# Thirteen pairs per feed-forward network as seven block products, with parts of 7, 8 and 7 pairs

## The chip, the cores and the metric

The kernel runs on one core of one Trainium2 chip. The metric is the time of one execution on the device in microseconds (us), as the median of several runs; smaller is better. The engines are TensorE (PE in the profile; its weight loads are PEld), VectorE (DVE), ScalarE (ACT), GpSimd (POOL) and SyncE (SP), which only issues transfers here. POOL issues transfers too.

## The reference

Two layers of a decoder trunk work on 16 meta tokens and 512 tokens, 528 rows of 1024 numbers, in float32. Each layer has a mixer (attention, a long and a short convolution from one input projection, then an output projection) and a feed-forward network (FFN):

```python
def ffn_sublayer(h, pre_g, post_g, w_up, conv_w, w_down):
    u = rms_norm(h, pre_g)
    z = jnp.einsum("bld,df->blf", u, w_up)        # 1024 -> 2 x 2816
    z = causal_depthwise_conv(z, conv_w)          # 3 taps
    g, up = jnp.split(z, 2, axis=-1)
    y = jnp.einsum("blf,fd->bld", jax.nn.silu(g) * up, w_down)
    return h + rms_norm(y, post_g)
```

At the end the meta tokens are removed. Only this part of the reference bears on the change; the mixer is `h += post_norm(w_out(head_norm(groups(w_in(pre_norm(h))))))`.

## The kernel before, in words

**Numbers as two halves.** Everything is held transposed: 128 features on the partitions, the 528 rows of the sequence along the free dimension. Each operand of a matmul is split into a high and a low half (hi by a cast on ACT, lo by a subtraction on DVE), and each product is three matmuls, hi by hi, hi by lo and lo by hi. `mm3` (L831) issues them.

**Weights.** `chunk_list` (L83) lists all weight blocks in the order of use. `prep_one` (L616) takes the next one: a load on SP's queue into a tile "raw", the cast (L652) and the subtraction (L653). `next_w` (L685) keeps two blocks ready beyond the one in use. The tiles whi and wlo have three buffers each. While the tile h isn't needed in the FFN, four pieces of it serve as further raw tiles (`raw_tile`, L570; the profile then names the tile h).

**The FFN.** The 2816 gate features and the 2816 up features are 22 pairs of blocks of 128. `PARTS` cuts the pairs into parts: after the up projection of a part's pairs comes the down product of that part, which multiplies the part's gated results by w_down and adds into yp (L2387 to L2415): eight output blocks m, the first two together and then one by one, each with (pairs of the part) x 3 x 2 matmuls in layer 0. The first down product's output is copied to yp by ACT (L2410), the second's added by DVE (L2412). The third is the function `finish`, together with the normalisation and the start of the next layer. Each pair's convolution, silu, product and split is `ffn_gate` (L2176).

**Ordinary pairs and seven pairs.** An ordinary pair multiplies two weight blocks (8 blocks of 128 x 128 each) by the whole u, in two halves of the sequence. A pair named in `SEVEN` is done by `seven_pair` (L2292) instead. Seen as 2 x 2 blocks (gate and up by the two halves of the 1024 features, and those by the two halves of the sequence), a pair is eight block products; with sums of the weights and of u, seven suffice. Each is four blocks deep, so 12 matmuls (`product`, L2284, with its matmul at L2288). The pair needs the weight parts w (the gate block itself), c and b (two sums each) and d (half a block): w and c go to whi and wlo, b to the tiles shi and slo, d to a pair of y tiles. shi and slo have one buffer each, in the pool tp (L2215). The products run in the order w, c, b, w, c, b, d (L2313 to L2333); the last is issued behind those of the next pair.

**Sums of u.** `normalised` (L2210) makes the normalised u and the four sums of it that the seven pairs need. It is a list of small steps with stops (`None`) in it: `build(5)` runs a few of them behind each ordinary pair of the first part, `build(99)` up to the next stop behind each output block of the first down product.

**Sums of weights.** They are made in DRAM ahead of time, at five places per layer, which `SUMS` lists: during the FFN of the layer before, during the layer's own mixer, during its FFN, and in its first and second down product. In the first three places a sum is `sum_steps` (L526): three copies from DRAM to DRAM on SP's queue and three accumulating transfers by POOL (L534). In the mixer, a planner (class `Flow`) orders all engines by estimated costs; the sums enter with the lowest priority, one each 40 us (L1846). In the FFN, `tick` (L2200) issues one step per pair. In the down products, `down_sum` (L581) loads the two blocks into h, adds on DVE (L593 to L596) and stores the result (L601).

**Blocks split ahead.** The first six weight blocks of layer 1's input projection are split in layer 0's FFN and stored in DRAM in halves, so that the transition between the layers needs only to fetch them. `store_one` (L661) takes the block that the call before has loaded, casts it to shi (L666), subtracts to slo (L667), stores both by POOL (L670), and loads the next block by SP (L675). There are seven calls, at the head of the pairs 8, 8, 9, 9, 10, 10 and 11 of layer 0.

**Order.** Mixer and transitions are written out by the planner. In the middle of the FFN a list scheduler orders each engine's instructions by its own estimate; an instruction that is ready may go ahead of an earlier one. `tc.issue_after(x)` holds what its block issues on the engine of x behind x, on that engine only.

## Time and profile before

| what | value |
|---|---|
| time, median of 3 runs | 1264.08 us (1263.58 to 1264.17) |
| time of the profiled execution | 1262.1 us |
| its span, first to last instruction | 1260.4 us |
| granted TensorE clock, mean | 0.999 |
| TensorE matmuls | 9554, of them 1764 in the products of seven pairs |
| DMA packets | 80755, 206.59 MB, mean 164 GB/s |

In the rows of the windows, each engine has its busy time in us and its number of instructions in brackets, in the order PE, PEld, DVE, ACT, POOL; then come the granted clock, the mean busy share of the 16 DMA engines and GB/s. In the rows of a timeline stand start, duration, engine, line, operation, what it writes and reads, and in square brackets the engine's idle time before it with what ended it. Some matmul records can be missing (a few per cent), so the number of matmuls in a window is a lower bound.

The FFN of layer 0 runs roughly from 276 to 640 us and that of layer 1 from 905 us to the end; the mixers lie before them. 1764 is the sum of the groups of L2288: 4 x 252 + 336 + 2 x 168 + 84, which is 21 pairs x 84.

### The profile page before, as it was taken

How to read it: one execution, taken by the hardware profiler on the slowest of the kernel's cores; microseconds unless marked ns; L12 is line 12 of the kernel's file. 1: busy time of each engine (PE TensorE's matmuls, PEld its weight loads, DVE VectorE, ACT ScalarE, POOL GpSimd, SP SyncE). 2: the span in 40 equal slices, each digit the busy share in tenths (PEclk: the TensorE clock that was granted, in tenths of full speed). 3: DMA queues.
4: the chain of work that ended last, by engine and by line, in shares of the span. 5: the costliest groups of instructions: out<-in, count | busy, mean ns of one | idle time of the engine just before them, and what ended most of it. 6: DMA issues, size and time to landing. Idle time of an engine off the chain costs nothing.

```text
span 1260.4 us, 24292 instructions
## 1 busy us (share of the span) xinstructions
PE 1244.2 (99%) x9554; PEld 1194.4 (95%) x9554; DVE 926.0 (73%) x1581; ACT 710.3 (56%) x1377; POOL 175.9 (14%) x360
## 2 busy tenths in 40 slices
PE   8999999999999999999999999999999999999997
PEld 8999898999999999999999988999999899989997
DVE  7887866589874776487688877756799748757954
ACT  7254576655444663476673545775554447526763
POOL 1323411001111001010003244110022000000000
PEclk9999999999999999999999999999999999999999
DMA  7267551726658755765652684547166565465611
GB/s 245 80 154 180 122 118 47 256 88 150 185 146 339 243 192 153 243 193 169 209 186 68 157 194 109 144 116 238 70 166 177 148 212 172 151 228 178 203 60 67
DMA packets 80755, 206.59 MB, mean 164 GB/s; under 512 B 8624, under 2 KB 18992, under 8 KB 80128
## 3 DMA queue, kind: packets, MB, share of 16 engines
q1 hardware_dynamic: 66976, 168.20, 42.1%
q0 software_dynamic: 13664, 36.84, 13.0%
q8 instruction: 75, 1.23, 0.4%
q14 instruction: 40, 0.33, 0.1%
HBM read 170.82 MB, written 50.60 MB: 176 GB/s over the span
## 4 chain that ended last, share of the span: by engine, by line
PE 94%; DVE 2%; ACT 1%; DMA 1%; POOL 1%; issue 0%; SPq 0%; DVEq 0%; ACTq 0%
PE psum L837 63%; PE psum L2288 17%; PE psum L1407 5%; PE psum L1671 3%; PE psum L1637 2%; PE psum L974 1%; PE psum L1593 1%; PE psum L1737 1%; PE psum L1323 1%; DMA raw<-in_w_dram 0%; POOL dm L1608 0%; DMA h<-in_x_dram 0%; DVE yp L1050 0%; DVE h L1060 0%; PE psum L1617 0%
## 5 line engine op out<-in xcount | busy, mean ns | idle before, releaser
L837 PE MATMUL psum<-y,whi 128*128 128x264 f32 (+3 forms) x1968 | 383.8, 299 | 0.8 <-DVE zs L989 0.7
L837 PEld LDWEIGHTS psum<-y,whi 128*128 128x128 f32 x1968 | 305.8, 188 | 13.7 <-DVE zs L989 0.9
L837 PE MATMUL psum<-uhi,whi 128*128 128x264 f32 (+1 forms) x1168 | 292.2, 289 | 1.5 <-ACT uhi L2069 0.8
L837 PE MATMUL psum<-ulo,whi 128*128 128x264 f32 (+1 forms) x1168 | 286.0, 284 | 0.6 <-DVE ulo L2071 0.4
L837 PE MATMUL psum<-uhi,wlo 128*128 128x264 f32 (+1 forms) x1168 | 285.3, 284 | 0.0
L837 PE MATMUL psum<-y,wlo 128*128 128x264 f32 (+3 forms) x984 | 274.0, 297 | 0.7 <-DVE wlo L793 0.7
L837 PEld LDWEIGHTS psum<-uhi,whi 128*128 128x128 f32 x1168 | 201.7, 189 | 5.9 <-issue 1.6
L837 PEld LDWEIGHTS psum<-ulo,whi 128*128 128x128 f32 x1168 | 201.8, 189 | 1.3 <-DVE ulo L2071 0.6
L837 PEld LDWEIGHTS psum<-uhi,wlo 128*128 128x128 f32 x1168 | 201.5, 189 | 0.0
L837 PEld LDWEIGHTS psum<-y,wlo 128*128 128x128 f32 x984 | 178.0, 188 | 6.4 <-DVE wlo L793 1.1
L2173 DVE SCALAR_TENSOR_TENSOR c<-zs,pv,c 128x528 f32<-128x528 f32 (+1 forms) x176 | 130.5, 756 | 21.2 <-ACT c L2171 19.9
L652 ACT CAST whi<-raw 128x1024 fp32r<-128x1024 f32 (+1 forms) x65 | 66.1, 1021 | 96.9 <-PE psum L837 74.3
L793 DVE TENSOR_TENSOR wlo<-raw,whi 128x1024 fp32r<-128x1024 f32 (+2 forms) x80 | 95.6, 1204 | 31.1 <-ACT whi L789 30.5
L789 ACT CAST whi<-raw 128x1024 fp32r<-128x1024 f32 (+2 forms) x80 | 81.7, 1030 | 26.3 <-PE psum L837 18.1
L653 DVE TENSOR_TENSOR wlo<-raw,whi 128x1024 fp32r<-128x1024 f32 (+1 forms) x65 | 76.9, 1183 | 20.9 <-ACT whi L652 20.9
L1153 DVE SCALAR_TENSOR_TENSOR cacc<-apad,pv,cacc 128x528 f32<-128x528 f32 x120 | 87.5, 771 | 0.1
L2288 PE MATMUL psum<-uhi,whi 128*128 128x258 f32 (+1 forms) x252 | 71.4, 284 | 0.0
L2288 PE MATMUL psum<-ulo,whi 128*128 128x258 f32 (+1 forms) x252 | 71.3, 283 | 0.0
L2288 PE MATMUL psum<-uhi,wlo 128*128 128x258 f32 (+1 forms) x252 | 70.8, 283 | 0.0
L2171 ACT ACTIVATE c<-zs,pv 128x528 f32<-128x528 f32 (+1 forms) x88 | 63.0, 727 | 6.8 <-DVE zs L2136 2.6
L2206 POOL COPY cols<-y 128x1 f32<-128x1 f32 x24 | 18.4, 767 | 334.7 <-ACT y L2187 334.4
L2288 PE MATMUL psum<-t,shi 128*128 128x258 f32 (+1 forms) x336 | 63.2, 283 | 0.0
(273 smaller groups left out, 2324.4 us busy)
## 6 DMA issues: line engine op xcount, KB each, us to landing
raw<-in_w_dram SPq DMA_DIRECT2D x114, 512.0 KB, 4.6
raw<-in_w_dram SPq DMA_DIRECT2D x30, 448.0 KB, 5.2
h<-in_w_dram SPq DMA_DIRECT2D x25, 512.0 KB, 4.7
raw<-w_sum SPq DMA_DIRECT2D x21, 512.0 KB, 5.2
h<-w_sum SPq DMA_DIRECT2D x21, 512.0 KB, 5.1
h<-in_w_dram POOLq DMA_DIRECT2D x16, 512.0 KB, 4.0
w_sum<-h POOLq DMA_DIRECT2D x16, 512.0 KB, 6.3
w_sum<-in_w_dram SPq DMA_DIRECT2D x26, 256.0 KB, 5.8
```

Source lines behind the costliest of these rows:

```text
L652: nc.scalar.copy(hi[:, :sz], raw[:, :sz])
L653: last_low[0] = nc.vector.tensor_sub(lo[:, :sz], raw[:, :sz], hi[:, :sz].bitcast(F32))
L789: nc.scalar.copy(box["hi"][:, :sz], box["raw"][:, :sz])
L793: nc.vector.tensor_sub(lo[:, :sz], box["raw"][:, :sz], box["hi"][:, :sz].bitcast(F32))
L837: nc.tensor.matmul(d, lhsT=w[a][:, k, cols], rhs=rhs(b, k, hf), start=start and i == 0 and p == 0, stop=stop and i == n - 1 and p == 2)
L1153: nc.vector.scalar_tensor_tensor(conv[j], in0=src, in1=conv[j], scalar=col("a_dw_w", CK * j + i), op0=ALU.mult, op1=ALU.add)
L1407: nc.tensor.matmul(ps[:n, :nw], lhsT=(uhi, ulo)[ui][:, k, P * b:P * b + n], rhs=w[wi][:, k % 4, :], start=k == 0 and p == 0, stop=k == KD ...
L1637: nc.tensor.matmul(s, lhsT=k[:, ka:ka + kn], rhs=q[:, s0:qz], start=i == 0, stop=i == 1)
L1671: nc.tensor.matmul(acc[:, s0 - qa:qz - qa], lhsT=vals[:, b].rearrange("p h d -> p (h d)")[:, o:o + P], rhs=box["p"], start=b == 0, stop=b ...
L2171: nc.scalar.activation(dst, src[:, 2:2 + 2 * fw], AF.Copy, scale=wtap(2, t))
L2173: nc.vector.scalar_tensor_tensor(dst, in0=src[:, i:i + 2 * fw], scalar=wtap(i, t), in1=dst, op0=ALU.mult, op1=ALU.add)
L2288: nc.tensor.matmul(psum[:, bank, :n7], lhsT=w[a][:, k0 + k, :], rhs=rhs(b, k), start=start and k == 0 and p == 0, stop=stop and k == K2 - ...
```

## The change

The parts become 7, 8 and 7 pairs. In both layers the pairs 7 to 13 and 15 to 20 become seven pairs, thirteen per layer; before there were nine in layer 0 (11 to 13, 15 to 20) and twelve in layer 1 (8 to 13, 15 to 20). So four ordinary pairs of layer 0 (7 to 10) and one of layer 1 (7) become seven pairs. Six sums are made in layer 0's mixer in place of three, four in layer 1's as before; they start at equal distances over 220 us (36.7 and 55 us). Each layer's FFN makes three sums of its own by `tick` in place of two. The seven calls of `store_one` move to the second down product of layer 0, one behind each group of output blocks: on DVE behind that block's addition, on SP's queue behind the last weight load. In `normalised`, one stop is left out when the first down product has been reached. The last edit keeps a list of eight y tiles right for a part of any size.

```diff
-PARTS = (8, 7, 7)
+PARTS = (7, 8, 7)
...
-SUMS = (((), (11, 12, 13), (15, 16), (17, 18), (19, 20)),
-        ((8, 9), (10, 11, 12, 13), (15, 16), (17, 18), (19, 20)))
+SUMS = (((), (7, 8, 9, 10, 11, 12), (13, 15, 16), (17, 18), (19, 20)),
+        ((7, 8), (9, 10, 11, 12), (13, 15, 16), (17, 18), (19, 20)))
...
-NEXT_SUMS, AHEAD_SPLITS = 13, (8, 8, 9, 9, 10, 10, 11)
-SUM_US, SUM_LAT, SUM_EVERY = 0.9, 9.0, 40.0
+NEXT_SUMS = 13
+SUM_US, SUM_LAT, SUM_SPAN = 0.9, 9.0, 220.0
...
-            tok = flow.op("sp", 2.0, copies, (Tok(flow.pe + SUM_EVERY * i),), prio=8, lat=SUM_LAT)
+            tok = flow.op("sp", 2.0, copies, (Tok(flow.pe + SUM_SPAN * i / len(sums_at(l, 1))),), prio=8, lat=SUM_LAT)
...
                     if k:
-                        yield None
+                        if not downs:
+                            yield None
                         yield lambda: block(0)
...
-            building = [None]
+            building, downs = [None], []
...
-                    for _ in range(AHEAD_SPLITS.count(f) if l == 0 else 0):
-                        store_one()
                     if f in seven:
...
+                downs.append(part)
                 if part < len(PARTS) - 1:
...
+                        if l == 0 and part == 1:
+                            with tc.issue_after(evac.ins), tc.issue_after(last_load[0].ins):
+                                store_one()
...
-                        raw = list(zip(*[g[f0 + k] for k in range(nf)], y_pair(nf)))
+                        raw = list(zip(*[g[f0 + k] for k in range(nf)], *[y_pair(k) for k in range(nf, KD)]))
```

## The prediction

> **What bounds the kernel now.** I read the page first, then busy time by windows of the two feed-forward parts, then TensorE's timeline for its gaps, and last the timelines of VectorE and GpSimd where the blocks are split ahead.
>
> ```profile
> span 1260.4 us, 24292 instructions
> PE 1244.2 (99%) x9554; PEld 1194.4 (95%) x9554; DVE 926.0 (73%) x1581; ACT 710.3 (56%) x1377; POOL 175.9 (14%) x360
> PE 94%; DVE 2%; ACT 1%; DMA 1%; POOL 1%; issue 0%; SPq 0%; DVEq 0%; ACTq 0%
> ```
>
> TensorE is the bound. Matmuls are pipelined, so "99%" alone would prove little, but the chain that ended last is 94% TensorE, and the windows show matmuls following at one constant distance:
>
> ```profile
> core 0: us, PE busy (x) PEld busy (x) DVE busy (x) ACT busy (x) POOL busy (x), PEclk, DMA share, GB/s
> 360.00:401.00 41.00, 41.00 (x340) 41.00 (x339) 23.88 (x28) 20.38 (x26) 4.86 (x9) 1.00 0.80 288
> 401.00:436.00 35.00, 35.00 (x289) 34.92 (x287) 22.84 (x27) 19.68 (x31) 3.73 (x7) 1.00 0.72 246
> 473.00:518.00 45.00, 45.00 (x373) 45.00 (x372) 27.06 (x35) 13.52 (x19) 5.10 (x8) 1.00 0.67 200
> 518.00:570.00 52.00, 52.00 (x431) 52.00 (x430) 39.30 (x51) 36.13 (x64) 4.66 (x5) 1.00 0.69 200
> 983.00:1023.00 40.00, 40.00 (x175) 32.31 (x174) 23.44 (x28) 17.28 (x24) 3.58 (x6) 1.00 0.64 196
> 1023.00:1072.00 49.00, 49.00 (x411) 49.00 (x409) 36.63 (x47) 34.73 (x62) 0.53 (x1) 1.00 0.55 169
> ```
>
> 360 to 401 is the first down product of layer 0 (with its head before 360), 401 to 436 ordinary pairs, 473 to 518 the second down product, 518 to 570 pairs made of seven products, and 983 to 1023 and 1023 to 1072 the first down product of layer 1 and the seven pairs behind it. The distance is 35/289 = 0.121 us for ordinary matmuls, 52/431 = 0.1207 us in layer 0's sevens and 49/411 = 0.119 us in layer 1's. So a matmul that is left out is worth 0.12 us wherever TensorE never waits.
>
> **What is removed.** An ordinary pair has 2 weight blocks x 8 x 3 x 2 halves = 96 matmuls, a seven pair 7 x 12 = 84. Layer 0 goes from 9 seven pairs to 13, layer 1 from 12 to 13. That is 4 x 12 x 0.1207 = 5.8 us and 12 x 0.119 = 1.4 us, together **-7.2 us**, if nothing else becomes late. The down products keep their matmuls: 22 blocks each way, only cut 7, 8, 7. The two priming matmuls per layer stay, and the last edit, the list of y tiles, gives the same tiles for 7 blocks.
>
> **What a seven pair costs beside TensorE.** It splits 3.5 weight blocks in place of two and empties its banks in six steps of ACT. In 518:570 DVE is busy 39.30 of 52 us and ACT 36.13, so a row of seven such pairs in layer 0 (7 to 13) keeps a quarter of DVE free; layer 1 already has six in a row without a gap of TensorE. I take 0. The building of the sums of u loses one ordinary pair to hide behind and moves four steps (two sums, two splits of 0.7 us a piece on DVE) into the first down product, which the dropped stop lets run as one group; layer 1 has seven pairs right behind that product, and TensorE is busy 40.00 of 40 and 49.00 of 49 us there. Also 0; a tile that comes late would cost the tenths by which it is late.
>
> **The sums of weights.** The mixer of layer 0 prepares six sums in place of three, layer 1 still four but 55 us apart. Each sum is three copies on SP's queue and three accumulating DMAs on POOL, behind which the attention's small POOL steps wait. TensorE's gaps in the two mixers:
>
> ```profile
> 115.56 0.39 PE L1617 MATMUL psum<-dm,ones_r 128*128 128x264 f32 x1 [0.43 <-POOL dm L1608]
> 136.25 0.51 PE L1671 MATMUL psum<-pf,vals 128*128 128x144 f32 x2 [0.28 <-POOL pf L1651]
> 185.70 1.13 PE L1323 MATMUL psum<-apad,bd 128*128 128x264 f32 x4 [0.38 <-ACT q L1619]
> 742.23 0.40 PE L1617 MATMUL psum<-dm,ones_r 128*128 128x264 f32 x1 [0.98 <-POOL dm L1608]
> 762.95 0.51 PE L1671 MATMUL psum<-pf,vals 128*128 128x144 f32 x2 [0.28 <-POOL pf L1651]
> 812.34 1.13 PE L1323 MATMUL psum<-apad,bd 128*128 128x264 f32 x4 [0.40 <-ACT q L1619]
> ...
> L534 POOL DMA_DIRECT2D w_sum<-w_sum x26: 796/844/890, 66.2 to 984.7; - x26
> L534 POOL DMA_DIRECT2D w_sum<-in_w_dram x13: 1176/1196/1244, 58.3 to 964.4; - x13
> ```
>
> Three sums go with gaps of 1.09 us, four with 1.66, so a sum costs at most 0.57 us: three more lie between 0 and 1.7 us, and the new spacing in layer 1 between -0.6 and +0.6. A sum holds POOL 1.20 + 2 x 0.84 us, and TensorE waited for POOL for a few tenths only. I take **+0.5 us**. The twelve small sum steps beside the pairs of each layer (eight before) are issued where POOL idles: 0.
>
> **The blocks split ahead.** This decides. Six blocks of layer 1's first projection are loaded, split into shi and slo, and stored. Both tiles have one buffer, and the third weight part of every seven pair ("b") takes the same two. Before, the six lay at 379 to 423, with three ordinary pairs behind them. Now each call sits in the second down product of layer 0; its DVE step is queued behind that output block's addition. The first call only loads, so the sixth split is behind the addition of the last output block, and b of pair 15 comes after it.
>
> ```profile
> 379.34 1.23 DVE L667 TENSOR_TENSOR slo<-h,shi 128x1024 fp32r<-128x1024 f32 x1 [2.20 <-ACT shi L666]
> 389.89 1.23 DVE L667 TENSOR_TENSOR slo<-raw,shi 128x1024 fp32r<-128x1024 f32 x1
> 399.86 1.23 DVE L667 TENSOR_TENSOR slo<-raw,shi 128x1024 fp32r<-128x1024 f32 x1 [4.25 <-DMA w_split<-slo]
> 407.88 1.23 DVE L667 TENSOR_TENSOR slo<-h,shi 128x1024 fp32r<-128x1024 f32 x1 [5.66 <-issue]
> 415.54 1.22 DVE L667 TENSOR_TENSOR slo<-raw,shi 128x1024 fp32r<-128x1024 f32 x1 [2.66 <-DMA w_split<-slo]
> 422.00 1.22 DVE L667 TENSOR_TENSOR slo<-h,shi 128x1024 fp32r<-128x1024 f32 x1
> ...
> 391.41 0.53 POOL L670 DMA_DIRECT2D w_split<-slo  x1 [0.73 <-DVE slo L667]
> 409.40 0.53 POOL L670 DMA_DIRECT2D w_split<-slo  x1 [5.03 <-DVE slo L667]
> ...
> DMA to landing us min/median/max: 4.4/6.5/8.4
> ...
> 515.21 1.22 DVE L642 TENSOR_TENSOR slo<-h,shi 128x1024 fp32r<-128x1024 f32 x1
> 518.32 0.70 DVE L2412 TENSOR_TENSOR yp<-yp,psum 128x528 f32<-128x528 f32 x1 [1.89 <-PE psum L837]
> ```
>
> The first six rows are the splits of slo, then stores of slo, the landing times of all stores of slo, the present split of b for pair 15, and the last addition. Splits follow each other after 10.5, 10.0, 8.0, 7.7 and 6.5 us, because the next waits for the store before it: 407.88 split, 409.40 store issued, 415.54 next split. Call this interval I. The down product gives one output block each 48 x 0.121 = 5.81 us, faster than any I in the trace.
>
> Let it start at 0; with 8 blocks of 48 matmuls it ends at 46.5. The first split follows the third addition: 17.4 + 0.8 = 18.2. Six intervals later (five splits and the sixth store) b of pair 15 can be written, 1.22 us more and it is there: 19.4 + 6I. I take I = 7.66, the last interval that a store alone set and after the down sums' own stores were out: 65.4, that is **18.9 us after the down product's end**. In the trace that split (515.21) ran three us before the end.
>
> What TensorE can do meanwhile: without b, pair 15 has four products, and pair 16 four. The order is the scheduler's, which fills in other matmuls where one is late:
>
> ```profile
> 457.87 1.21 PE psum L2288 x10
> 459.09 1.46 PE psum L837 x12
> 460.55 1.69 PE psum L2288 x14
> ```
>
> Here an ordinary pair's matmuls (L837) run between products of a seven pair. So I grant all eight products, 96 x 0.1207 = 11.6 us (5.8 if it grants only pair 15's). The stall is 18.9 - 11.6 = **+7.3 us**, in general 6I - 38.7. Behind the waiting DVE step stand the low halves of the weights of pair 16 and the last additions; behind POOL's stores nothing urgent. For I = 6.46 the stall is 0, for the mean of the five, 8.53, it is 12.5.
>
> The page "DMA: Bandwidth & Descriptors" of the Trainium skill (Anatomy of one DMA) fits a GpSimd DMA as 2.0 us plus bytes over 436e3 per us: 3.2 us, an estimate for 512 KB. The trace's stores of slo take 4.4 to 8.4, so this case disagrees under load; by the page the chain would keep pace and the sum be the first rival's.
>
> **The sum.** -7.2 + 0.5 + 7.3 = +0.6 us. The profiled execution took 1262.1 us (span 1260.4), 2.0 below the median of 1264.08; so 1262.7 on its scale and **1264.7** on the median's. A measurement here can tell about 0.2%, 2.5 us, from no change.
>
> **The rivals.** First, the cover holds. If stores land sooner, so that I is under 7.15, the stall is under 4.2 and the gain shows; with no stall, -7.2 + 0.5 = -6.7: 1257.4. For it: one store of shi landed early,
>
> ```profile
> DMA to landing us min/median/max: 3.0/6.4/8.4
> ```
>
> and the last interval was 6.5. Against it: DMA share is 0.67 in 473:518 before any block is there, and 0.80 in 360:401 with half of them.
>
> Second, slower: TensorE's order holds only pair 15's own four products ahead of b, because the scheduler believes the stores faster, or the low halves for pair 16 stand on DVE behind the sixth split. Then cover is 5.8, the stall 18.9 - 5.8 = 13.1, the change +6.4: 1270.5. The same sign comes with I over 8.0 at full cover; that is the point from which it decides. For it: in the trace DVE does stand idle for a store (4.25, 2.66 us) with other work behind.
>
> Third, a stall also restarts TensorE slowly, as at the program's start:
>
> ```profile
> 1.26 7.87 PE L2034 MATMUL psum<-warm 128*128 128x264 f32 x44 [1.26 <-DVE warm L2032]
> ...
> 1253.25 2.00 PE L1081 MATMUL psum<-yp,ident 128*128 128x256 f32 x8 [1.38 <-DVE yp L1050]
> ```
>
> 44 matmuls took 7.87 us in place of 44 x 0.121 = 5.3, so 2.5 us more: with the forecast's stall in one piece +3.1, 1267.2. The longest gap inside the program is 1.38 us, so how it restarts after a longer one isn't shown. The page "TensorE: Matmul & The Clock Gate" of the Trainium skill (Part 1) says that idling for about 3.4 us halves the clock; no run here shows that.
>
> Fourth, the change doesn't do what it says: the seven pairs would have DVE as their bound and give nothing. 39.30 of 52 us speaks against it. Then DVE's slack, 12.7 of 52 us, would have to be gone; without gain and without stall it is +0.5, 1264.6.
>
> **How the numbers follow.** Forecast, a stall that about eats the gain: 0.37; its own range, I from 7.0 to 8.1, is 1260.7 to 1267.3, with 0.03 beyond the bound on each side. Cover holds: 0.33. Slower by little cover or long intervals: 0.24. Slow restart: 0.04. Sevens without gain: 0.02, counted as same. Faster 0.33 + 0.03 = 0.36; slower 0.24 + 0.04 + 0.03 = 0.31; same 0.31 + 0.02 = 0.33. The range of 8 in 10 runs from the whole gain, 1257, to the second rival with some tenths, 1271.
>
> **What would show it.** Right: TensorE has 60 matmuls fewer at 0.12 us; in layer 0, directly behind the second down product, a gap of 5 to 9 us in one or two pieces, ended by DVE's split of b (L642), with splits L667 some 8 us apart and the last one after the down product's end; mixers' gaps together under 4 us. Wrong: no gap there over 2 us (the first rival), over 12 us (the second), matmuls at twice the distance behind the gap (the third), or a gap at the first seven pairs of layer 0, in a mixer, or in layer 1, which I put at nothing.

## The result, and the profile after

The changed kernel takes 1285.18 us, median of 4 runs (1282.70 to 1285.72), where the kernel before took 1264.12 us beside it: the ratio is 1.0163, with an interval of 1.0146 to 1.0181. It is slower by some 21 us; forecast was no change that could be told (1264.7, at most 1271).

The profiled execution took 1285.67 us. Its page, from the top: span, busy time by engine, the granted clock in forty slices, and the chain that ended last by engine.

```profile
span 1284.0 us, 24337 instructions
...
PE 1247.4 (97%) x9494; PEld 1193.3 (93%) x9494; DVE 937.6 (73%) x1595; ACT 723.3 (56%) x1405; POOL 192.8 (15%) x383
...
PEclk9999999999999999899999999989999999999999
...
PE 82%; DMA 5%; DVE 5%; issue 4%; ACT 2%; POOL 1%; SPq 0%; DVEq 0%; POOLq 0%; ACTq 0%
```

Three things are to be seen. The matmuls are 9554 - 9494 = 60 fewer, as the change says. TensorE's share of the chain falls from 94% to 82%, and DMA, DVE and "issue" take what it lost. And the clock falls below full speed in two slices of 32 us, the 17th (514 to 546) and the 27th (835 to 867): two places to look at.

Where the time went is read from four stages. The border of each is the first matmul of a group of L974, the sums of squares of a normalisation, at the end of a mixer or of an FFN: A ends with the last group in layer 0's mixer, B with the first group behind layer 0's FFN, C with the first group at the end of layer 1's mixer, and D is the rest (the end of that mixer, and layer 1's FFN).

| profiled execution of | A | B | C | D | span |
|---|---|---|---|---|---|
| the kernel before | 275.4 | 344.0 | 252.4 | 388.6 | 1260.4 |
| the changed kernel | 276.5 | 359.0 | 261.8 | 386.7 | 1284.0 |

B lost 15.0 us although it has 48 matmuls fewer, C lost 9.4, of which D gives 1.9 back (the planner orders the end of the mixer otherwise), and A is within what it varies by between executions (274.9 to 278.0 in all the kernels below).

**Stage B, behind the second down product.** The windows of the changed kernel: the product itself, the 41 us around and behind its end (514.4), and two stretches behind gaps.

```profile
core 0: us, PE busy (x) PEld busy (x) DVE busy (x) ACT busy (x) POOL busy (x), PEclk, DMA share, GB/s
467.00:514.00 47.00, 47.00 (x388) 46.80 (x387) 26.32 (x32) 13.02 (x17) 8.80 (x15) 1.00 0.79 260
...
509.00:550.00 41.00, 30.02 (x198) 28.01 (x197) 16.67 (x18) 16.18 (x24) 3.19 (x6) 0.88 0.78 280
...
531.00:537.00 6.00, 5.86 (x26) 5.55 (x27) 3.55 (x3) 2.31 (x3) 0.53 (x1) 0.52 0.75 290
...
545.40:550.00 4.60, 4.12 (x20) 3.91 (x21) 3.48 (x4) 3.35 (x6) 0.00 (x0) 0.67 1.04 382
```

The product itself runs without a wait. In 509 to 550 TensorE did 198 matmuls where 41/0.1207 = 340 fit: 142 x 0.1207 = 17 us lost there. Cut where b arrives (below), the stretch behind the product is

```profile
514.38:539.85 25.47, 17.32 (x112) 15.95 (x110) 10.75 (x10) 9.62 (x14) 2.66 (x5) 0.87 0.71 249
539.85:550.00 10.15, 7.32 (x42) 6.68 (x43) 5.45 (x7) 5.51 (x9) 0.00 (x0) 0.85 0.84 293
```

so 12 us are lost up to b (112 matmuls where 211 fit) and 5 us behind it (42 where 84 fit). The gaps of TensorE's timeline in the changed kernel, here and in layer 1's mixer:

```profile
516.61 0.52 PE L2289 MATMUL psum<-t,whi 128*128 128x264 f32 x2 [0.62 <-ACT whi L641]
517.87 0.39 PE L2289 MATMUL psum<-t,wlo 128*128 128x264 f32 x1 [0.74 <-DVE wlo L642]
524.77 0.39 PE L2289 MATMUL psum<-uhi,whi 128*128 128x264 f32 x1 [1.04 <-ACT psum L2315]
530.99 0.81 PE L2289 MATMUL psum<-t,whi 128*128 128x264 f32 x2 [4.48 <-ACT whi L641]
539.87 0.39 PE L2289 MATMUL psum<-t,slo 128*128 128x264 f32 x1 [1.14 <-DVE slo L642]
545.44 0.52 PE L2289 MATMUL psum<-t,whi 128*128 128x264 f32 x2 [1.91 <-ACT whi L641]
...
854.63 1.70 PE L1671 MATMUL psum<-pf,vals 128*128 128x400 f32 x2 [3.47 <-POOL pf L1651]
859.45 0.82 PE L1671 MATMUL psum<-pf,vals 128*128 128x272 f32 x1 [2.06 <-POOL pf L1651]
```

The six gaps shown from 516 to 546 add up to 9.9 us. The stall isn't one wait for b: three of the gaps are for the cast of a weight part (L641). Behind two of them the clock is 0.52 and 0.67: 26 matmuls in 6 us where 50 fit and 20 in 4.6 us where 38 fit, another 5 us. But TensorE still had to wait 1.14 us for b at 539.87, so what it lost ahead of that, by gaps or by the slow clock, lies inside the wait for b.

VectorE's timeline in the same kernel shows the chain of the six splits, and the split of b of pair 15:

```profile
485.86 1.22 DVE L667 TENSOR_TENSOR slo<-raw,shi 128x1024 fp32r<-128x1024 f32 x1
...
496.92 1.23 DVE L667 TENSOR_TENSOR slo<-raw,shi 128x1024 fp32r<-128x1024 f32 x1 [1.91 <-DMA w_split<-slo]
...
505.40 1.22 DVE L667 TENSOR_TENSOR slo<-raw,shi 128x1024 fp32r<-128x1024 f32 x1
...
517.73 1.22 DVE L667 TENSOR_TENSOR slo<-raw,shi 128x1024 fp32r<-128x1024 f32 x1
...
525.08 1.22 DVE L667 TENSOR_TENSOR slo<-raw,shi 128x1024 fp32r<-128x1024 f32 x1
...
534.10 1.23 DVE L667 TENSOR_TENSOR slo<-raw,shi 128x1024 fp32r<-128x1024 f32 x1 [0.77 <-DVE wlo L653]
538.59 1.23 DVE L642 TENSOR_TENSOR slo<-h,shi 128x1024 fp32r<-128x1024 f32 x1 [3.27 <-DMA w_split<-slo]
```

From the first split to that of b six links take 52.7 us, 8.8 each; b is there at 539.82, 25.4 us behind the product's end. Five of the six links end within 0.2 us of the landing of the last store of slo (496.85, 505.31, 524.90, 534.02 and 538.51 in the trace). The step at 517.73 comes 3.3 us behind its landing (514.42): it stood on VectorE behind the split of a weight part that was late itself. ScalarE's timeline shows why weights are late too:

```profile
500.77 1.05 ACT L652 CAST whi<-raw 128x1024 fp32r<-128x1024 f32 x1 [8.73 <-DMA raw<-in_w_dram]
...
511.85 1.05 ACT L666 CAST shi<-raw 128x1024 fp32r<-128x1024 f32 x1 [6.34 <-DMA w_split<-shi]
515.51 1.05 ACT L641 CAST whi<-h 128x1024 fp32r<-128x1024 f32 x1 [2.61 <-DMA h<-w_sum]
...
529.89 1.04 ACT L641 CAST whi<-raw 128x1024 fp32r<-128x1024 f32 x1 [1.64 <-DMA raw<-w_sum]
```

A block's cast (511.85) sits at the head of ScalarE's queue until the store of the last block has landed, and all casts behind it wait; weight loads themselves arrive late (8.73). The longest gap of TensorE, 4.48 us, is such a load: the cast at 529.89 waits for a part that SyncE requested only at 525.19.

```profile
518.98 0.33 SPq L631 DMA_DIRECT2D raw<-in_w_dram  x1
...
525.19 0.53 SPq L631 DMA_DIRECT2D raw<-w_sum  x1
```

The profile names as the end of SyncE's wait before 518.98 the fourth block's split (517.73 to 518.95), and before 525.19 the split of the part that was loaded at 518.98 (done at 525.16). So the waiting blocks also hold raw tiles, and the loads behind them go out late. Of the stores of slo the view of that tile says

```profile
DMA to landing us min/median/max: 2.9/7.1/9.5
```

against 4.4, 6.5 and 8.4 before.

**Stage C, layer 1's mixer.** GpSimd's timeline in the changed kernel, where the fourth sum's accumulating transfers (L534) meet attention's steps (L1651):

```profile
844.75 1.17 POOL L534 DMA_DIRECT2D w_sum<-in_w_dram  x1 [3.59 <-DMA w_sum<-in_w_dram]
...
853.41 0.85 POOL L534 DMA_DIRECT2D w_sum<-w_sum  x1 [6.02 <-issue]
853.99 0.58 POOL L1651 TENSOR_SCALAR_AFFINE_SELECT pf<-pf 128x128 f32<-128x128 f32 x1
858.26 0.83 POOL L534 DMA_DIRECT2D w_sum<-w_sum  x1 [3.69 <-DMA w_sum<-w_sum]
858.81 0.82 POOL L1651 TENSOR_SCALAR_AFFINE_SELECT pf<-pf 128x128 f32<-128x128 f32 x2
```

An L534 waits for the transfer before it to land and keeps GpSimd standing; attention's L1651 is next in the queue, ready, and is released only behind it. These are the two gaps of 3.47 and 2.06 us above. The rest of the 9.4 us goes with a slow clock behind them:

```profile
855.00:860.00 5.00, 2.94 (x8) 1.94 (x8) 1.46 (x3) 0.91 (x3) 1.38 (x3) 0.50 0.41 50
860.00:865.00 5.00, 5.00 (x26) 4.63 (x24) 1.88 (x5) 2.21 (x6) 0.19 (x1) 0.56 0.38 56
```

At 55 us per sum the fourth follows close behind the third and its three transfers are issued one behind the other at the end of attention. In the kernel before, at 40 us, the fourth's three (818.26, 831.47 and 837.53) also lay between attention's steps, but each came when the one before it had landed (825.18 and 836.96), and GpSimd stood idle for 0.1 us at most ahead of them.

### The profile page after: what moved, and what is told of

It reads as the page before. It is cut to its first block, busy times and chain, and to the rows that moved or that the text cites. A ratio compares the mean times of both kernels' runs of the same rounds, so it can differ in the third digit from the quotient of the medians.

```text
span 1284.0 us, 24337 instructions
## 1 busy us (share of the span) xinstructions
PE 1247.4 (97%) x9494; PEld 1193.3 (93%) x9494; DVE 937.6 (73%) x1595; ACT 723.3 (56%) x1405; POOL 192.8 (15%) x383
## 4 chain that ended last, share of the span: by engine, by line
PE 82%; DMA 5%; DVE 5%; issue 4%; ACT 2%; POOL 1%; SPq 0%; DVEq 0%; POOLq 0%; ACTq 0%
PE psum L837 51%; PE psum L2289 18%; PE psum L1407 4%; PE psum L1671 3%; PE psum L1637 2%; DMA w_split<-slo 1%; PE psum L974 1%; DMA h<-in_w_dram 1%; PE psum L1593 1%; DVE c L2173 1%; DMA w_sum<-in_w_dram 1%; PE psum L1737 1%; DMA w_sum<-h 1%; DVE wlo L793 1%; PE psum L1323 1%
## 5 line engine op out<-in xcount | busy, mean ns | idle before, releaser
L837 PE MATMUL psum<-uhi,whi 128*128 128x264 f32 (+1 forms) x1008 | 256.6, 289 | 0.9 <-ACT uhi L2069 0.8
L837 PE MATMUL psum<-ulo,whi 128*128 128x264 f32 (+1 forms) x1008 | 250.8, 284 | 0.5 <-DVE ulo L2071 0.4
L837 PE MATMUL psum<-uhi,wlo 128*128 128x264 f32 (+1 forms) x1008 | 250.3, 283 | 0.0
L837 PEld LDWEIGHTS psum<-uhi,whi 128*128 128x128 f32 x1008 | 175.6, 188 | 4.9 <-issue 1.6
L837 PEld LDWEIGHTS psum<-ulo,whi 128*128 128x128 f32 x1008 | 175.7, 188 | 1.2 <-DVE ulo L2071 0.6
L837 PEld LDWEIGHTS psum<-uhi,wlo 128*128 128x128 f32 x1008 | 175.6, 188 | 0.0
L652 ACT CAST whi<-raw 128x1024 fp32r<-128x1024 f32 (+1 forms) x60 | 60.7, 1015 | 88.9 <-PE psum L837 64.3
L2289 PE MATMUL psum<-uhi,whi 128*128 128x264 f32 (+1 forms) x312 | 89.2, 286 | 2.5 <-ACT whi L652 1.4
L2289 PE MATMUL psum<-ulo,whi 128*128 128x264 f32 (+1 forms) x312 | 88.7, 285 | 0.0
L2289 PE MATMUL psum<-uhi,wlo 128*128 128x264 f32 (+1 forms) x312 | 87.6, 285 | 0.0
L653 DVE TENSOR_TENSOR wlo<-raw,whi 128x1024 fp32r<-128x1024 f32 (+1 forms) x60 | 70.6, 1177 | 16.7 <-ACT whi L652 15.4
L2289 PE MATMUL psum<-t,shi 128*128 128x264 f32 (+1 forms) x416 | 78.7, 284 | 1.1 <-ACT zs L2323 0.5
L2206 POOL COPY cols<-y 128x1 f32<-128x1 f32 x32 | 22.7, 709 | 368.0 <-ACT y L2187 367.7
```

Of the source, the lines that this page charges most:

```text
L652: nc.scalar.copy(hi[:, :sz], raw[:, :sz])
L653: last_low[0] = nc.vector.tensor_sub(lo[:, :sz], raw[:, :sz], hi[:, :sz].bitcast(F32))
L837: nc.tensor.matmul(d, lhsT=w[a][:, k, cols], rhs=rhs(b, k, hf), start=start and i == 0 and p == 0, stop=stop and i == n - 1 and p == 2)
L2289: nc.tensor.matmul(psum[:, bank, :n7], lhsT=w[a][:, k0 + k, :], rhs=rhs(b, k), start=start and k == 0 and p == 0, stop=stop and k == K2 - ...
```

## The experiments

Theory: two separate mechanisms make the loss, the chain of blocks in the second down product (stage B) and the fourth sum of layer 1 (stage C); the sevens themselves gain. Main rival: pairs as seven, sums and blocks together bring more transfers than this stretch can carry, and no single part is to blame. The stages of the profiled execution of each kernel, its median, and the ratio on record of its runs to those of the kernel before on the same chip:

| kernel | A | B | C | D | median | ratio (interval) |
|---|---|---|---|---|---|---|
| l1_spacing_40 | 276.0 | 359.9 | 252.1 | 389.5 | 1279.68 | 1.0129 (1.0112 to 1.0145) |
| before_l1_spacing_55 | 276.1 | 344.1 | 261.5 | 387.6 | 1271.45 | 1.0063 (1.0048 to 1.0078) |
| no_blocks | 274.9 | 338.8 | 271.6 | 390.4 | 1276.90 | 1.0104 (1.0082 to 1.0125) |
| no_blocks_spacing_40 | 278.0 | 338.9 | 259.6 | 389.8 | 1267.67 | 1.0033 (1.0020 to 1.0047) |
| before_blocks_in_down | 276.8 | 367.2 | 252.9 | 388.8 | 1286.46 | 1.0181 (1.0166 to 1.0196) |
| early_chain_40 | 277.4 | 348.6 | 255.2 | 389.8 | 1269.17 | 1.0034 (1.0017 to 1.0051) |
| three_blocks_40 | 276.7 | 342.7 | 264.2 | 386.6 | 1272.06 | 1.0076 (1.0054 to 1.0097) |
| blocks_before_sevens_40 | 275.7 | 348.8 | 253.7 | 389.7 | 1267.88 | 1.0037 (1.0024 to 1.0050) |
| two_tiles_40 | 275.6 | 345.2 | 253.0 | 390.7 | 1270.98 | 1.0059 (1.0035 to 1.0084) |
| early_own_raw_40 | 277.1 | 348.0 | 252.5 | 391.5 | 1269.44 | 1.0044 (1.0029 to 1.0059) |
| early_two_tiles_40 | 275.5 | 347.0 | 252.6 | 389.7 | 1266.54 | 1.0030 (1.0018 to 1.0043) |
| spread_two_tiles_40 | 275.1 | 344.7 | 256.9 | 391.3 | 1268.08 | 1.0032 (1.0010 to 1.0053) |
| three_and_three_40 | 276.8 | 343.5 | 252.6 | 389.9 | 1264.61 | 1.0006 (0.9993 to 1.0018) |
| four_and_two_40 | 277.0 | 341.5 | 253.3 | 389.5 | 1261.67 | 0.9985 (0.9972 to 0.9997) |
| four_and_two_12_sevens | 275.4 | 342.6 | 252.2 | 388.8 | 1265.00 | 1.0014 (1.0000 to 1.0029) |
| four_early_40 | 275.7 | 338.7 | 255.1 | 391.8 | 1262.87 | 0.9998 (0.9979 to 1.0017) |

The stages are of one execution each. Where the stall is only partly gone, a kernel's runs lie far apart (two_tiles_40 1266 to 1282), and a profiled execution may lie some us off its median.

### Layer 1's spacing

```diff
# l1_spacing_40, on the changed kernel
-(Tok(flow.pe + SUM_SPAN * i / len(sums_at(l, 1))),)
+(Tok(flow.pe + (40.0 * i if l else SUM_SPAN * i / len(sums_at(l, 1)))),)
# before_l1_spacing_55, on the kernel before
-(Tok(flow.pe + SUM_EVERY * i),)
+(Tok(flow.pe + (55.0 if l else SUM_EVERY) * i),)
```

> The changed kernel, with layer 1's four sums 40 us apart again (layer 0's six as changed). Theory of the late sum: at 55 us apart the fourth sum falls into the end of layer 1's attention, where POOL waits for its transfers in front of the attention's own POOL steps; the two gaps of TensorE at 854 and 859 us and the halved clock around them go, about -8.5 us, so near 1276.7 us; the gaps behind the second down product of layer 0 stay. Rival, that the whole of the added traffic (221 in place of 207 MB) slows the mixers: no change, 1285 us within 2.

> The kernel before, with nothing changed but layer 1's four sums, 55 us apart in place of 40. Late sum: the loss shows by itself, +8.5 us, so near 1272.6 us, with a gap of TensorE of some 5 us before L1671 in layer 1's mixer that POOL ends. Rival, total traffic: that is the same as before, so 1264 us within 2.

Undone, the spacing gives 5.5 us back where 8.5 were expected: stage C is the old one (252.1, 9.7 less), but D is 2.8 longer. Put alone into the kernel before, it costs 8 us, as expected, with the same gaps in TensorE's timeline of that kernel:

```profile
839.30 0.94 PE L1671 MATMUL psum<-pf,vals 128*128 128x400 f32 x2 [2.62 <-POOL pf L1651]
...
843.95 1.27 PE L1671 MATMUL psum<-pf,vals 128*128 128x272 f32 x2 [3.15 <-POOL pf L1651]
```

This half is settled: it has nothing to do with sevens or blocks.

### The blocks, taken out and put alone

```diff
# no_blocks: no block is split ahead; layer 1's mixer splits them
-MASK = "111111000000000000000000"
+MASK = "000000000000000000000000"
# no_blocks_spacing_40: this and l1_spacing_40
# before_blocks_in_down, on the kernel before
-NEXT_SUMS, AHEAD_SPLITS = 13, (8, 8, 9, 9, 10, 10, 11)
+NEXT_SUMS, AHEAD_SPLITS = 13, ()
...
+                        if l == 0 and part == 1:
+                            with tc.issue_after(evac.ins), tc.issue_after(last_load[0].ins):
+                                store_one()
```

> The changed kernel without any blocks split ahead: the six blocks of layer 1 are loaded and split in the transition between the layers like the others. Theory of the block chain (each split waits for the store before it, and b of pair 15 waits for the last): the gaps behind the second down product go, -17 to -20 us in layer 0's feed-forward part; the transition splits six blocks more, 0 to +8 us; so 1265 to 1276 us. Rival, that the seven pairs' own weights and sums come late there for lack of transfer bandwidth: gaps of over 5 us stay behind that product, and the time is over 1278 us.

> Both edits together: no blocks split ahead, layer 1's sums 40 us apart. If block chain and late sum are the whole loss and add up, this is the run without blocks less 8.5 us, 1257 to 1267 us, and layer 0's feed-forward part shows the whole gain of the four seven pairs, 5.8 us against the kernel before. If they share a cause, it is more than 3 us off that sum.

> The kernel before, with one part of the change alone: its six blocks are split in the second down product instead of in pairs 8 to 11; parts, sums and sevens stay as before. Theory (the chain of blocks, together with the traffic of the two sums made there, holds back the low half of b of pair 15 and the weights behind it, whatever the first sevens do): layer 0's FFN loses about what it lost in the changed kernel, 359.0 - 338.9 = 20 us between the kernels with and without blocks, so about 1264 + 20 = 1284 us, 1278 to 1288, with the gaps of TensorE behind the second down product. Rival (the loss needs the six sums or the seven block products at 7 to 10 beside it): under 1270 us.

Without blocks stage B is 338.8 us, 5.2 below the kernel before, and in the same 41 us of its windows TensorE doesn't wait:

```profile
509.00:550.00 41.00, 41.00 (x341) 41.00 (x340) 28.93 (x37) 26.33 (x45) 2.21 (x3) 1.00 0.64 192
```

Both times came out just above what was expected (1276.90 us against 1265 to 1276, and with the spacing undone 1267.67 against 1257 to 1267). The whole was above the kernel before all the same, since stage C pays for blocks that are not there (259.6 against 252.1 us at equal spacing): what the blocks buy is about 7 us. The chain alone, in the kernel before with its nine sevens and three sums, costs 23 us, and its timeline of TensorE has the same gaps, the longest again for a weight part's cast:

```profile
511.25 1.18 PE L837 MATMUL psum<-y,whi 128*128 128x264 f32 x4 [2.34 <-ACT whi L652]
...
539.77 0.59 PE L2288 MATMUL psum<-t,whi 128*128 128x264 f32 x1 [4.51 <-ACT whi L641]
...
548.54 0.39 PE L2288 MATMUL psum<-t,slo 128*128 128x264 f32 x1 [1.05 <-DVE slo L642]
...
554.18 0.51 PE L2288 MATMUL psum<-t,whi 128*128 128x264 f32 x2 [1.99 <-ACT whi L641]
```

So the main rival falls for the cause of the loss: neither the new sevens nor the new sums are needed for it.

### What in the chain holds: length, place, tiles

All with layer 1's spacing of 40 us.

```diff
# three_blocks_40
-MASK = "111111000000000000000000"
+MASK = "111000000000000000000000"
# early_chain_40: seven calls, three at the head of pair 14
+                    for _ in range((14, 14, 14).count(f) if l == 0 else 0):
+                        store_one()
...
-                        if l == 0 and part == 1:
+                        if l == 0 and part == 1 and m < 5:
# early_own_raw_40: this, and in store_one
-            raw = raw_tile()
+            raw = T(wp, [P, CHUNK], F32, "raw", 3)
# two_tiles_40, in store_one
-            hi, lo = (T(tx[0], [P, 2 * SB], F32R, t) for t in ("shi", "slo")) if sz <= 2 * SB else ...
+            hi, lo = T(tx[0], [P, 2 * SB], F32R, ("shi", "slo")[len(stored) % 2]), raw
# early_two_tiles_40: early_own_raw_40 and two_tiles_40
```

> The changed kernel with layer 1's spacing of 40 us and three blocks in place of six (the other three are split in layer 1's mixer, as in the kernel without blocks). Theory (length of the chain): three links fewer, 29 us, so b of pair 15 is ready before the product ends and the whole 20 us of layer 0's FFN come back; the three blocks that are not split ahead cost up to half of the 7.2 us that transition and layer 1's mixer lost without blocks at this spacing (36.9 + 222.7 against 34.7 + 217.4 us): 1279.7 - 20 + 3.6 = 1263 us (1259 to 1266). Rival (traffic of sums and weights, of which the blocks are only a part): 1268 us or more.

> The changed kernel with layer 1's spacing of 40 us, and the chain of blocks begun earlier: three calls in pair 14, ahead of the second down product, and four behind its first output blocks (seven calls, as many as before). Theory (a chain with links of about 9.65 us that begins too late): two links lie ahead of the product, so the last split ends some 20 us earlier, b of pair 15 is ready about 5 us behind the product, which the 11.6 us of products that need no b cover: layer 0's FFN 359.9 to about 340 us, time 1279.7 - 20 = about 1260 us (1257 to 1264), below the kernel before. Rival (not the chain but the traffic of blocks, sums and weights together holds everything back; the same bytes are moved within 10 us of the same place): a gap of over 5 us stays, 1268 us or more.

> early_chain_40 again (three calls in pair 14, four behind the first output blocks of the second down product), with the blocks' raw weights always in the raw tiles of their own and not in the tiles of the residual, where a sum's load overwrote one of them. Expected as there for the time: the stall behind the product is gone, a smaller one lies in the product's first half, where the blocks' waits now stand ahead of the product's own weights; layer 0's FFN about 348 us (348.6 in early_chain_40), time 1265 to 1270 us. If the place of the raw weights matters to the stall, 1263 or less.

> The changed kernel with layer 1's spacing of 40 us; each block's high half lies in the one and the other of the two tiles in turn, and its low half is written over its raw weights, so that a block's cast waits for the store of the block two before it and not for the last one. Same blocks, same bytes, same places. Theory (the stall comes from the two tiles: each link of the chain is a store that must land, and casts of weights stand behind a waiting block's cast on ScalarE): links of half the length, most of the 20 us of layer 0's FFN come back: 359.9 to under 346 us, time under 1266 us. Rival (traffic: 300 to 400 GB/s in this stretch, raw weights and sums land late whatever the tiles do): layer 0's FFN over 352 us, time over 1271 us.

> early_own_raw_40 and two_tiles_40 together: the chain begins in pair 14 and has two links in flight. Theory (tiles): no stall behind the product and a smaller one in it, layer 0's FFN 339 to 344 us, time 1257 to 1262 us, below the kernel before. Rival (traffic): as early_own_raw_40, 1266 us or more.

In early_chain_40 a sum's load overwrites one block's raw weights before they are split (early_own_raw_40 mends that); its work and its bytes are the same, and so is its time.

Three links fewer took 17 of the 21 us out of stage B, as the length of the chain says; stage C lost 12 where 3.6 was expected, and D gave 3 of them back: 1272 us, above the border of the rival, but for stage C and not for stage B. Why three unsplit blocks cost stage C more than six do (12 against 7.5) was not tried. Two tiles, with every block and byte in its place, took 8.7 us off the median and 14.7 off stage B of its profiled execution, which is the fastest of its ten runs. That is the expected side of the tiles' theory for stage B, though the median (1271) lies on the border that was set. An earlier start took 10 us off the median where 20 were expected, and both together 13: early_chain_40 (1269) and early_two_tiles_40 (1267) lie on the side that was set for the rival, though the gap of over 5 us that it foretold for early_chain_40 isn't there. So stores that must land before a tile is free are a good part of the some 21 us in stage B; that they are the larger part only the fastest execution of two_tiles_40 shows. The rival is not dead: no variant that keeps six blocks around the second product got stage B under 345 us, where 339 is possible. What was left lay mostly in the product itself, now in front of its own weights. Timelines of TensorE and ScalarE in early_own_raw_40:

```profile
502.29 0.75 PE L837 MATMUL psum<-y,whi 128*128 128x264 f32 x4 [2.97 <-ACT whi L652]
...
500.25 1.04 ACT L666 CAST shi<-raw 128x1024 fp32r<-128x1024 f32 x1 [9.62 <-DMA w_split<-shi]
```

and of two_tiles_40:

```profile
503.68 1.98 PE L837 MATMUL psum<-y,whi 128*128 128x264 f32 x7 [2.38 <-ACT whi L652]
...
502.58 1.05 ACT L652 CAST whi<-raw 128x1024 fp32r<-128x1024 f32 x1 [4.11 <-DMA raw<-in_w_dram]
```

Both gaps end with the cast of a weight of the product. In early_own_raw_40 that cast (501.20) stands on ScalarE directly behind a block's (500.25), which waits for the block's tile to be stored. In two_tiles_40 it waits for its load, which SyncE issued at 494.88, when a store out of that raw tile had landed (8.8 us behind its issue); the load itself took 7.6 us more. So two tiles move the wait for a store from shi and slo to the raw tiles, and what the slow transfers add of their own these runs don't tell apart.

### Out of the product

All with layer 1's spacing of 40 us.

```diff
# blocks_before_sevens_40: calls at pairs 3, 3, 4, 4, 5, 5, 6, none in the product
+                    for _ in range((3, 3, 4, 4, 5, 5, 6).count(f) if l == 0 else 0):
+                        store_one()
# spread_two_tiles_40: two_tiles_40; calls at 3, 4, 5, 6 (the last loads nothing) and, in the product,
-                        if l == 0 and part == 1:
+                        if l == 0 and part == 1 and m < 4:
# three_and_three_40: the same calls with m < 5, tiles as in the changed kernel
# four_and_two_40: calls at 3, 4, 5, 5, 6 (the last loads nothing), m < 4
# four_early_40: the same calls, none in the product, four blocks in MASK
# four_and_two_12_sevens: four_and_two_40 and
-SUMS = (((), (7, 8, 9, 10, 11, 12), (13, 15, 16), (17, 18), (19, 20)),
-        ((7, 8), (9, 10, 11, 12), (13, 15, 16), (17, 18), (19, 20)))
+SUMS = (((), (8, 9, 10, 11, 12), (13, 15, 16), (17, 18), (19, 20)),
+        ((8, 9), (10, 11, 12), (13, 15, 16), (17, 18), (19, 20)))
```

> The changed kernel with layer 1's spacing of 40 us, and the six blocks split in pairs 3 to 6 (calls 3, 3, 4, 4, 5, 5, 6), ordinary pairs ahead of the first pair as seven, in place of the second down product. Theory (there the two tiles are free and no pair as seven waits for them): the 20 us of layer 0's FFN come back, about 1260 us (1256 to 1264). Rival (there the raw weights have three tiles only, shared with the pairs' own weights, and ScalarE and VectorE make the operands of the sevens at the same time): gaps in pairs 3 to 7 of over 6 us together, 1266 us or more.

> The changed kernel with layer 1's spacing of 40 us, two tiles as in two_tiles_40, three blocks split in pairs 3 to 6 and three behind the first four groups of the second down product. Both theories take the bytes of the product's stretch to be lower by half of the blocks, and both say that the stall behind the product is small (three blocks there alone left 342.7 us); what is tried is whether pairs 3 to 6 take three blocks for nothing, where seven calls cost about 10 us: if so layer 0's FFN is under 343 us and the time 1257 to 1261 us; if not (they wait for the raw tiles that the pairs' own weights use), over 346 us and 1264 us or more.

> The changed kernel with layer 1's spacing of 40 us; three blocks split in pairs 3 to 6 and three in the second down product (four calls), the tiles as in the changed kernel. Theory (a): the three in pairs 3 to 6 are free, the three in the product cost what three_blocks_40 showed (342.7 - 338.9 = 4 us), transition and layer 1's mixer are as in the kernel before: 276 + 342.7 + 34.8 + 217.4 + 378.3 and 10.9 behind it = 1260 us span, time 1262 us (1259 to 1265). If pairs 3 to 6 are not free: 1266 us or more.

> As three_and_three_40 with four blocks in pairs 3 to 6 and two in the product (three calls). Theory (a): one link fewer behind, no stall at the product's end: layer 0's FFN 340 to 342 us, time 1258 to 1262 us. If the fourth block in pairs 3 to 6 costs: gaps at pairs 4 to 7, 1265 us or more.

> four_and_two_40 with pair 7 as an ordinary pair in both layers: twelve pairs as seven block products per FFN, 24 matmuls more (2.9 us at 0.12 us each), and one ordinary pair between the first down product and the first seven. Theory (b) (the first seven behind the product waits and loses its gain): no wait at the first seven, so within 1.5 us of four_and_two_40, or faster. Rival (its wait of 1 to 1.7 us is all): slower by about 2 us.

> As four_and_two_40 with four blocks only, all in pairs 3 to 6, and none in the second down product; the other two are split in layer 1's mixer. Tells what the product's two blocks cost from what pairs 3 to 6 cost: if pairs 3 to 6 are free, layer 0's FFN is that of the kernel without blocks (338.9 us), and transition and layer 1's mixer lose 2 to 10 us (7.2 us with none of six split ahead at this spacing, 11.8 with three): 1259 to 1266 us. If they are not, layer 0's FFN over 342 us.

In spread_two_tiles_40 the product has three calls (m = 1, 2, 3) and not the four that its expectation counts on, so five blocks are split and the sixth is loaded in vain; layer 1's mixer splits that one. Its time (1268.08 us) is on the side that was set for "not free", but with one block missing and stage B between the two borders (344.7) it says little beyond its neighbours.

Pairs 3 to 6 take four blocks for nothing: with four_early_40 stage B is 338.7 us, that of the kernel without blocks. Six are too many there (1267.88 us, the rival's side). TensorE's timeline of blocks_before_sevens_40:

```profile
337.33 0.51 PE L837 MATMUL psum<-y,whi 128*128 128x264 f32 x2 [1.91 <-ACT whi L652]
...
400.30 0.39 PE L2289 MATMUL psum<-uhi,whi 128*128 128x264 f32 x1 [4.27 <-ACT whi L652]
```

Two blocks in the second product cost 2.8 us more (341.5), three 4.8 (343.5), and both spare stage C some of what the unsplit blocks cost it. four_and_two_40 is the best layout found: 1261.67 us, 0.15% below the kernel before, with an interval that stays just under 1. It is the lowest of many layouts tried, so a gain that small isn't certain. three_and_three_40 (1264.61) came out at the upper end of its expectation, four_early_40 (1262.87) in the middle.

The timeline of TensorE in four_and_two_40 shows what is left, a short wait at each place:

```profile
326.38 0.48 PE L837 MATMUL psum<-uhi,whi 128*128 128x264 f32 x2 [1.43 <-DVE zs L2136]
...
519.44 0.39 PE L2289 MATMUL psum<-uhi,whi 128*128 128x264 f32 x1 [0.46 <-ACT whi L652]
...
1015.33 0.39 PE L2289 MATMUL psum<-uhi,whi 128*128 128x258 f32 x1 [0.99 <-ACT whi L652]
```

The last one is the wait of the sevens right behind the first down product of layer 1. With pair 7 as an ordinary pair it is not there, and stage D is 388.8 us against 389.5: 12 matmuls more and no time lost. In layer 0 the same edit lost 1.1 us of 1.4. But the median of that kernel is 3.3 us above four_and_two_40, on the rival's side of its expectation, and its one profile doesn't explain that: it is of the fastest of its ten runs (span 1259.0), the other's of one 1.4 us above its median (1261.3). So that the thirteenth seven of layer 1 gains nothing is read from these stages alone and not shown.

## Why the prediction was wrong, step by step

**The matmuls removed.** 60 fewer, at 0.12 us. Layer 0's 5.8 us came out as 5.2 once the blocks were out of the way. Layer 1's 1.4 us came in part at most: stage C and D together are 641.6 us with the spacing undone, against 641.0 before, but at 55 us D is 386.7 against 387.6 in before_l1_spacing_55. "TensorE is busy 40.00 of 40 and 49.00 of 49 us there. Also 0" was read from a kernel in which an ordinary pair stood between the product and the sevens. In the changed kernel it held: no gap is to be seen there. In nearly all kernels with the spacing undone the sevens wait for a weight at that place, 0.6 us in l1_spacing_40 and up to 1.7 in others.

**The sums of weights, +0.5.** For layer 0 right as far as it can be read. For layer 1's spacing "between -0.6 and +0.6" was wrong by a power of ten: 5.5 us when undone, 8 when put alone into the kernel before. The failed step was the bound. It shared out gaps that existed evenly over the sums, so it priced a sum where it already lay. What decides is where a moved sum lands: its accumulating transfers wait on GpSimd for each other, and whatever of attention is queued behind them waits along. The list of what is queued behind that wait was in the text as "attention's small POOL steps", but not followed to the place at which the fourth sum would arrive.

**The blocks, +7.3.** The mechanism was found at the right place: two tiles, a chain of stores, the first split 18.3 us into the product, which begins at 467.58 (18.2 forecast), the last one behind its end, all eight products of pairs 15 and 16 used as cover and one of pair 17 with them. Two terms failed. The first is the link: it is 8.8 us and not 7.66, which by the prediction's own formula gives 6 x 8.8 - 38.7 = 14 in place of 7.3; with the ninth product it is 13, and 12 were measured up to b. Its mean of five intervals, 8.53, would have been the better value, as the forecast took the one interval that was free of the sums' stores into a stretch that begins with such stores, and left out that a step may also stand behind another weight's. The second is what lies behind b, which was put at nothing: 5 us up to 550, where the next part was requested at 539.84, when b's split was done, and its cast made a gap of 1.91 us, and where the clock, the third rival (0.04, +3.1), fell to 0.67 for 4.6 us (about 2 us). Some 3 us more were lost elsewhere in the stage, most of it up to 620. The cover was not free of waits either, as the forecast had counted it: its own weight part c came late, since the blocks hold the raw tiles and the places in the engines' order (the second rival had named that order for DVE). This and the first slow stretch of the clock cost nothing of their own, as TensorE had to wait for b behind them. In the changed kernel the stage lost 15.0 + 5.2 = 20 us to the blocks, and the same blocks alone cost the kernel before 23.

**The price of a store.** The 3.2 us that "DMA: Bandwidth & Descriptors" of the Trainium skill gives for such a store is close to the best case of this trace (2.9), not to its median (7.1).

**The chances.** The rivals were kept apart as alternatives. The runs show them together: a long link, a late cover and a slow clock came in one stall.

## What to carry to other kernels

A step that takes a single-buffered tile and ends in a store costs a store's landing per use, and it holds back every instruction behind it on ScalarE and VectorE, other weights' casts too, and the loads that wait for its raw tile; count the links, and put them where nothing that shares the tile is due soon and where the transfer queues have room. A low-priority job with waits of its own, moved on an in-order engine, is priced by what stands behind it at its new place and not by what it cost at the old one. And when a saving leaves TensorE with fewer matmuls per weight block, look at the first such pair behind a stretch that loaded other weights.

## What the runs showed of the hardware

The clock falls behind gaps that are shorter and less regular than I had expected. In the changed kernel it was 0.52 for 6 us behind a gap of 4.48 us and 0.67 over 4.6 us behind one of 1.91. Windows of two_tiles_40 behind a gap of 2.38 us (ending at 503.68) and behind one of 1.68 us (at 1018.46):

```profile
503.00:508.00 5.00, 4.32 (x23) 4.31 (x24) 4.11 (x4) 2.52 (x3) 0.00 (x0) 0.66 1.05 394
...
1019.00:1021.00 2.00, 1.59 (x12) 1.57 (x13) 2.00 (x3) 2.00 (x4) 0.00 (x0) 1.00 0.18 36
```

and of four_early_40 behind one of 1.60 us at the same place of the program (1014.01):

```profile
1016.00:1020.00 4.00, 4.00 (x23) 4.00 (x22) 4.00 (x6) 2.60 (x6) 0.00 (x0) 0.57 0.63 213
```

So a gap of 1.6 us may halve the clock for some us and one of 1.7 may not. "TensorE: Matmul & The Clock Gate" of the Trainium skill (Part 1) says that activity is judged in windows of about 3.4 us that run on their own, not from the gap's start; that a gap's length alone doesn't decide agrees with these rows. It also has the clock halved by a whole idle window; these rows show it halved behind 1.60 and 2.38 us, which is less. What a stall costs here is its gaps and, where nothing else is waited for, the slow stretch behind them: about 2 us behind b in stage B, and in stage C some 1.5 and 2.2 us, estimated from TensorE's 2.94 and 5.00 busy us at 0.50 and 0.56. The gaps there leave 9.4 - 3.47 - 2.06 = 3.9 us to explain.
